# First stage of an encoder layer on one core: constant products ahead, squares behind the first parts, the norm's sums a block later

## The chip, the core and the metric

The kernel runs on one core of a Trainium2 chip. Its engines run at the same time and wait for each other through semaphores: TensorE (PE in the views, with its weight loads as PEld), VectorE (DVE), ScalarE (ACT), GpSimd (POOL) and SyncE (SP), which issues nearly all transfers. The metric is the time of one execution on the device in microseconds (us); lower is better.

## What is computed

One layer of a hybrid encoder on x of 1024 frames by 1024 features, in float32. The start of it is all that this study needs:

```python
h = rmsnorm(x, norm_mix_g[li])          # x * rsqrt(mean(x*x) + EPS) * gain
z = h @ w_in[li]
qa, fa, ia, ga, qb, kb, vb, gate_a, gate_b = jnp.split(z, split_at, axis=-1)
oa = hgrn2_mixer(qa, fa, ia, ga, lower_bounds[li], hgrn_onorm_g[li])
ob = band_attention(qb, kb, vb, ...)
```

Behind it follow the two branches' projections, a SwiGLU block and a gated embedding, which the change leaves as they are.

## The kernel before

x lies with its features on the 128 partitions: eight chunks of 128 features by 1024 frames. Every float32 factor of a large product is cut in two parts, a first part `hi` (rounded, from ACT) and a rest `lo` (the value minus its first part, from DVE for x, from POOL for weights), and a product is made of three: hi x hi, lo x hi and hi x lo. A weight tile of 128 x 1024 passes through `unit` and `unit_piece`: load into a raw buffer (two of them), cast on ACT (`wh`), subtraction on POOL (`wl`); four pairs of `wh` and `wl` go round, and a new tile must wait until TensorE has left the oldest.

`first_norm` is the first stage. It loads the eight chunks and two weight tiles (of q and f of the first head), the tiles in two pieces of 256 and 768 columns. For each chunk ACT makes the first part scaled by the norm's gain (`self.A.activation`), DVE the rest (`split`, L194; for the first chunk in two halves, L281). The norm's own factor, one number per frame, is not needed yet: it is put on the results afterwards. For it ACT squares each chunk in place (`norm_feed`) and DVE adds the squares up in `self.acc` (L204). TensorE makes 8 chunks x 4 results x 3 = 96 products of 512 columns, chunk by chunk, into four banks of PSUM (`outs`), whose pool has eight.

`hgrn_in(0, outs)` follows. Its eight token blocks of 24 products each (256 columns, PE tiles `pm<-wh,s` and `pm<-wl,s`) take two further weight tiles (`in_tm`). `norm_sums` sums `acc` over the partitions with 8 products against a column of ones, DVE scales, and POOL takes the power -1/2 (L215), which gives `self.r`, one factor per frame. Each block's result is then scaled by `r` (L338 and L340 on DVE, L339 on ACT), which frees its bank. `norm_rows` spreads `r` over the partitions with 8 products against the unit matrix, ACT copies them to `rb`, and `rows_out` scales the four waiting results. `near` then makes products of q and f which the mixer needs behind the next head's first products.

The order on each engine is the order in which the code issues, arranged by a scheduler for DVE, POOL and ACT where the code doesn't pin it (`Pinned`, `order`): TensorE, SP and the instructions sent through `self.A`, `self.V` and `self.G` are pinned. Helpers record one line for all that they issue: L81 is every product of `mul`, L76 every load, L52 every pinned instruction, L121 and L124 the cast and the subtraction of `unit_piece`.

Of the kernel before, what the change touches and what calls it, by code (L numbers as in the profile page):

```python
# [13 lines left out]
AF = mybir.ActivationFunctionType  # L14
ALU = mybir.AluOpType
AX = mybir.AxisListType

P = 128
# [8 lines left out]

SLOTS = 32
LATE = 8
FIRST = 4  # L30
RING = 4
RAW = 2
# [7 lines left out]
def f32(ap):  # L40
    return ap.bitcast(F32)
# [13 lines left out]
class Trunk:  # L55
# [205 lines left out]
    def first_norm(self):  # L261

        nc = self.nc
        self.u = []
        outs = [self.mm() for _ in range(4)]
        start = [self.unit() for _ in range(2)]
        ws = [(hi, lo) for hi, lo, _, _ in start]
        for k in range(KC):
            x = self.slot()
            sc = self.cols[:, C_MIX + k:C_MIX + k + 1]  # L270
            if k == 0:

                hi, lo = self.slot(F32R), self.slot(F32R)
                h0, h1 = slice(0, HALF), slice(HALF, T)
                self.load(x[:, h0], self.d["x"][k][:, h0])
                for unit in start:
                    self.unit_piece(unit, 0, 2 * P)
                self.load(x[:, h1], self.d["x"][k][:, h1])
                for h in (h0, h1):
                    self.A.activation(hi[:, h], x[:, h], AF.Copy, scale=sc)  # L280
                    nc.vector.scalar_tensor_tensor(lo[:, h], x[:, h], sc, f32(hi[:, h]), ALU.mult, ALU.subtract)  # L281
                self.u.append((hi, lo))
            else:
                self.load(x, self.d["x"][k])
                self.u.append(self.split(x, sc, self.A))
            if k == 1:
                for unit in start:
                    self.unit_piece(unit, 2 * P, D)
            if k == 3:
                self.load(self.eye, self.d["eye"])  # L290
                self.load(self.masks, self.d["masks"])
            if k:
                self.norm_feed(prev, k == 1, prev, act=self.A)
            prev = x
        self.norm_feed(prev, False, prev, act=self.A)
        self.lower_bound()
        pairs = [self.feature_pairs(ws[i // 2], self.u, i % 2) for i in range(4)]
        for k in range(KC):
            for i in (0, 2, 1, 3):
                ah, al, bh, bl = pairs[i][k]  # L300
                self.mul(outs[i], ah, bh, start=k == 0, stop=False)
                self.mul(outs[i], ah, bl, start=False, stop=False)
                self.mul(outs[i], al, bh, start=False, stop=k == KC - 1)
        return outs


    def hgrn_in(self, h, outs=None):

        nc = self.nc
        q, f, v, g = self.hg[h] = [self.slot() for _ in range(4)]  # L310

        def rows_out(j, half, ps):
            hs = slice(half * HALF, half * HALF + HALF)
            if j == 0:
                nc.vector.scalar_tensor_tensor(q[:, hs], ps, 128.0 ** -0.5, self.rb[:, hs], ALU.mult, ALU.mult)
            else:
                nc.vector.tensor_tensor(f[:, hs], ps, self.rb[:, hs], ALU.mult)
                nc.scalar.activation(f[:, hs], f[:, hs], AF.Sigmoid)
                nc.vector.tensor_scalar(f[:, hs], f[:, hs], self.lb1[:, h:h + 1], self.lb[:, h:h + 1], ALU.mult, ALU.add)

        if outs is None:
            for j in range(2):
                (w,) = self.weights()
                for half in range(2):
                    ps = yield from self.feature(w, self.u, half, piece=3)
                    rows_out(j, half, ps)
                    yield 1296
            near = self.near(h)
        else:
            near = iter(())  # L330
        ws = self.weights(2)
        for b in range(8):
            ps = yield from self.token(ws, b, 256, piece=4)
            if outs is not None and b == 0:
                self.norm_sums()
            bs = slice(b * P, b * P + P)
            r = self.r[:, b:b + 1]
            nc.vector.tensor_scalar(v[:, bs], ps[:, :P], r, None, ALU.mult)  # L338
            nc.scalar.activation(g[:, bs], ps[:, P:256], AF.Sigmoid, scale=r)  # L339
            nc.vector.scalar_tensor_tensor(g[:, bs], ps[:, P:256], r, g[:, bs], ALU.mult, ALU.mult)  # L340
            if outs is not None and b == 1:
                self.norm_rows()
                for i in range(4):
                    rows_out(i // 2, i % 2, outs[i])
                near = self.near(h)
            next(near, None)
            yield 1296

    def near(self, h):

        nc = self.nc
        q, f = self.hg[h][:2]
        kt = self.slot()
        self.V.tensor_scalar(kt, f, -1.0, 1.0, ALU.mult, ALU.add)
        parts = []

        def product(a, b, tag):
            hi, lo = [self.small(HALF, F32R, tag=tag, shape=(P, HALF if tag == "qk" else 640)) for _ in range(2)]
            raw = self.small(640, tag="s")
            self.V.tensor_tensor(raw[:, :HALF], a, b, ALU.mult)  # L360
            parts.append((hi[:, :HALF], lo[:, :HALF], raw[:, :HALF]))

        def part(hi, lo, raw):
            nc.scalar.copy(hi, raw)
            nc.gpsimd.tensor_tensor(lo, raw, f32(hi), ALU.subtract)

        for i in range(2):
            hs = slice(i * HALF, i * HALF + HALF)
            product(kt[:, hs], q[:, hs], "qk")
        yield  # L370
        for i in range(2):
            part(*parts[i])
        yield
        self.V.tensor_tensor(q, q, f, ALU.mult)
        yield
        qv, kv = (t[:, :].rearrange("p (j two) -> p j two", two=2) for t in (q, kt))
        product(kv[:, :, 0], qv[:, :, 1], "bias")
        yield
        yield
        part(*parts[2])  # L380
        self.hg[h] += [kt, parts]
# [248 lines left out]
    def attention(self):  # L630
# [32 lines left out]

        for i in range(FIRST, 8):
            next(feed, None)
            if i == FIRST:
                self.hgrn_gate()
# [809 lines left out]
    def run(self):  # L1477
# [16 lines left out]
        with ExitStack() as es:  # L1494
# [13 lines left out]
            with ExitStack() as mixer:  # L1508
# [5 lines left out]
                self.feed = self.attn_in()  # L1514
                weave(chain(self.attn_v(), islice(self.feed, FIRST)), self.hgrn_mix(3), 41500 + 1300 * FIRST, 17000)
                self.attn_setup()
# [11 lines left out]
            with ExitStack() as xs:  # L1528
                self.late = xs.enter_context(tc.tile_pool(name="late", bufs=LATE, reuse_waits="tile"))
                self.sq = Small(tc, xs, {"square": 1}, "out_", reuse_waits="tile")  # L1530
# [29 lines left out]
def drain(stream):  # L1560
    while True:
        try:
            next(stream)
        except StopIteration as e:
            return e.value


def weave(main, side, main_ns, side_ns):

    done = {id(main): 0, id(side): 0}  # L1570
    live = {id(main): (main, main_ns), id(side): (side, side_ns)}
    while live:
        i = min(live, key=lambda i: done[i])
        stream, whole = live[i]
        got = next(stream, None)
        if got is None:
            del live[i]
        else:
            done[i] += max(got, 50) / whole
# [94 lines left out]
```

## Time and profile before

| what | value |
|---|---|
| three runs | 1618.75 us median, 1617.07 to 1619.6 |
| the profiled execution | 1616.41 us, its span 1614.6 us |
| TensorE busy | 1592.5 us, 99% of the span |
| DVE, ACT, POOL busy | 1095.5, 589.6, 677.2 us |
| mean granted TensorE clock | 0.998 |

The span runs from the first to the last instruction of the profiled execution; the time beside it holds 1.8 us more, for what lies around the program. The profiled execution is 2.3 us below the median of the three runs, so a sum made from its trace gives a difference, which is then taken from the median. Matmuls are pipelined: the time from start to start tells their pace, their own length is longer.

### The profile page before, as it was taken

Reading aid. Unit: us, or ns where it says so; the run is one execution under the profiler, and the core shown is the slowest. Engines: PE = TensorE matmul, PEld = TensorE weight load, DVE = VectorE, ACT = ScalarE, POOL = GpSimd, SP = SyncE. Lnnn points to the kernel's source line nnn. Section 1 sums busy time; section 2 is a strip of 40 time slices with the busy share of each in tenths; the row PEclk is TensorE's granted clock in tenths of the full one; section 3 lists DMA queues with packets and bytes.
Section 4 is the critical chain, followed back from the end, with each engine's and each line's share of the span. In section 5 each row is a group of like instructions: output and inputs, shape, how many; then the busy total and the mean of one; then the engine's idle time right before and its main releaser. Section 6 shows DMA issues by size and latency. Waiting matters only on the chain.

```text
span 1614.6 us, 21560 instructions
## 1 busy us (share of the span) xinstructions
PE 1592.5 (99%) x8356; PEld 1333.0 (83%) x8356; DVE 1095.5 (68%) x1706; ACT 589.6 (37%) x999; POOL 677.2 (42%) x362
## 2 busy tenths in 40 slices
PE   8999999999999999999999999999999999999998
PEld 6998998878888888888887788888888888888887
DVE  5656655389897443334988888888888856437653
ACT  5221121277776311121466423222222235336321
POOL 3422221313122122125322777777777765546320
PEclk9999999999999999999999999999999999999999
DMA  5101000200103475733343432232333277655511
GB/s 188 53 27 53 27 27 27 85 1 27 60 14 107 152 235 185 257 133 131 105 143 145 147 114 98 98 98 98 107 103 113 82 271 281 211 195 176 196 72 53
DMA packets 64471, 189.62 MB, mean 117 GB/s; under 512 B 7280, under 2 KB 8048, under 8 KB 62448
## 3 DMA queue, kind: packets, MB, share of 16 engines
q1 hardware_dynamic: 64224, 188.22, 33.9%
q8 instruction: 66, 1.08, 0.3%
q14 instruction: 37, 0.30, 0.1%
q10 hardware_dynamic: 144, 0.02, 0.0%
HBM read 139.71 MB, written 48.50 MB: 117 GB/s over the span
## 4 chain that ended last, share of the span: by engine, by line
PE 83%; DVE 8%; ACT 2%; DMA 1%; issue 1%; POOL 1%; SPq 0%; DVEq 0%; ACTq 0%; POOLq 0%
PE pm L81 80%; DVE s L52 5%; PE pm L84 3%; DVE m L52 2%; ACT s L52 1%; POOL wl L124 1%; DMA wr<-in_sg 0%; DMA wr<-d 0%; ACT wh L121 0%; DVE q L52 0%; DMA wr<-in_su 0%; DVE wl L124 0%; ACT m L52 0%; DMA wr<-in_qk 0%; POOL m L547 0%
## 5 line engine op out<-in xcount | busy, mean ns | idle before, releaser
L81 PE MATMUL pm<-s,wh 128*128 128x512 f32 (+1 forms) x2136 | 659.8, 390 | 6.2 <-ACT wh L121 5.1
L124 POOL TENSOR_TENSOR wl<-wr,wh 128x1024 fp32r<-128x1024 f32 (+2 forms) x114 | 285.0, 2504 | 533.7 <-ACT wh L121 526.1
L81 PEld LDWEIGHTS pm<-s,wh 128*128 128x128 f32 x2136 | 398.2, 188 | 89.0 <-ACT wh L121 5.1
L81 PE MATMUL pm<-s,wl 128*128 128x512 f32 (+1 forms) x1068 | 415.0, 389 | 0.5 <-POOL wl L124 0.5
L81 PE MATMUL pm<-s,whi 128*128 128x512 f32 x1232 | 386.0, 394 | 5.1 <-ACT whi L52 2.1
L81 PEld LDWEIGHTS pm<-s,whi 128*128 128x128 f32 x1232 | 233.0, 189 | 58.6 <-ACT whi L52 2.6
L52 DVE TENSOR_TENSOR s<-s,s 128x512 f32<-128x512 f32 (+3 forms) x172 | 208.4, 1238 | 76.8 <-ACT s L52 42.1
L121 ACT CAST wh<-wr 128x1024 fp32r<-128x1024 f32 (+2 forms) x120 | 121.3, 1011 | 377.4 <-PE pm L81 188.3
L81 PE MATMUL pm<-s,wlo 128*128 128x512 f32 x616 | 243.3, 395 | 0.3 <-DVE wlo L52 0.3
L81 PE MATMUL pm<-wh,s 128*128 128x256 f32 (+1 forms) x896 | 238.2, 340 | 0.0
L81 PEld LDWEIGHTS pm<-s,wl 128*128 128x128 f32 x1068 | 200.7, 188 | 42.7 <-POOL wl L124 1.4
L81 PEld LDWEIGHTS pm<-wh,s 128*128 128x128 f32 x896 | 154.5, 190 | 13.9 <-DVE s L340 0.2
L81 PE MATMUL pm<-wl,s 128*128 128x256 f32 (+1 forms) x448 | 147.5, 329 | 0.8 <-POOL wl L124 0.8
L81 PEld LDWEIGHTS pm<-s,wlo 128*128 128x128 f32 x616 | 116.6, 189 | 27.2 <-DVE wlo L52 0.7
L52 DVE TENSOR_TENSOR s<-pm,s 128x512 f32<-128x512 f32 x101 | 65.7, 686 | 81.0 <-PE pm L81 81.0
L52 POOL TENSOR_TENSOR s<-s,t 128x512 f32<-128x512 f32 x44 | 75.5, 1716 | 89.8 <-ACT t L52 89.8
L52 DVE TENSOR_TENSOR t<-pm,t 128x512 f32<-128x512 f32 x106 | 72.8, 687 | 53.1 <-PE pm L81 50.0
L52 ACT CAST whi<-q 128x512 fp32r<-128x512 f32 (+1 forms) x63 | 47.8, 759 | 155.3 <-DVE q L52 133.2
L52 POOL TENSOR_TENSOR wlo<-wr,whi 128x512 fp32r<-128x512 f32 (+1 forms) x46 | 93.2, 2033 | 25.8 <-ACT whi L52 25.1
L81 PEld LDWEIGHTS pm<-wl,s 128*128 128x128 f32 x448 | 85.3, 191 | 6.3 <-POOL wl L124 1.0
L52 ACT CAST s<-s 128x1024 fp32r<-128x1024 f32 x70 | 69.1, 1004 | 57.6 <-DMA s<-d 23.2
L547 POOL TENSOR_TENSOR m<-m,mhalf 128x8 f32<-128x8 f32 x16 | 26.6, 1664 | 122.8 <-DVE m L52 122.7
(136 smaller groups left out, 1881.2 us busy)
## 6 DMA issues: line engine op xcount, KB each, us to landing
s<-d SPq DMA_DIRECT2D x51, 512.0 KB, 5.0
d<-s SPq DMA_DIRECT2D x87, 256.0 KB, 2.5
d<-dq SPq DMA_DIRECT2D x60, 256.0 KB, 4.6
wr<-d SPq DMA_DIRECT2D x28, 512.0 KB, 3.6
wr<-in_fm SPq DMA_DIRECT2D x22, 512.0 KB, 3.5
dq<-in_wq SPq DMA_DIRECT2D x11, 1024.0 KB, 7.1
wr<-in_sg SPq DMA_DIRECT2D x22, 512.0 KB, 3.9
wr<-in_su SPq DMA_DIRECT2D x22, 512.0 KB, 4.3
```

Source lines behind the costliest of these rows:

```text
L52: return lambda *a, **k: self.trunk.order(op(*a, **k), self.key)
L81: return self.order(self.nc.tensor.matmul(*a, **k))
L84: return self.order(self.nc.tensor.transpose(*a, **k))
L121: self.nc.scalar.copy(hi[:, c], raw[:, c])
L124: rest.tensor_tensor(lo[:, c], raw[:, c], f32(hi[:, c]), ALU.subtract)
L547: nc.gpsimd.tensor_tensor(ss, ss, self.mhalf[:, 0:8], ALU.pow)
```

## The change

Three things change, all in the first 60 us. Ahead of everything TensorE issues 18 products of a constant tile of ones (128 columns each) into a bank of their own. The squares and their adds are issued behind all eight first parts and rests, and the load, cast and subtraction of the next two weight tiles (`weights(0, ahead=2)`) ahead of them. In `hgrn_in(0, outs)` the sums of the norm are issued behind token block 1 in place of block 0, the scaling of blocks 0 and 1 behind that, and the norm's rows behind block 3 in place of block 1; the steps of `near`, one for each block from there, are emptied at the end.

```diff
+IDLE = 18
@@ first_norm
-        self.u = []
+        self.u, xs = [], []
+        idle = self.mm()
+        for _ in range(IDLE):
+            self.mul(idle[:, :P], self.onesr, self.onesr, start=True, stop=True)
         outs = [self.mm() for _ in range(4)]
...
-            if k:
-                self.norm_feed(prev, k == 1, prev, act=self.A)
-            prev = x
-        self.norm_feed(prev, False, prev, act=self.A)
+            xs.append(x)
+        self.weights(0, ahead=2)
+        for k, x in enumerate(xs):
+            self.norm_feed(x, k == 0, x, act=self.A)
         self.lower_bound()
@@ hgrn_in
         ws = self.weights(2)
+        made = []
         for b in range(8):
             ps = yield from self.token(ws, b, 256, piece=4)
-            if outs is not None and b == 0:
+            if outs is not None and b == 1:
                 self.norm_sums()
-            bs = slice(b * P, b * P + P)
-            r = self.r[:, b:b + 1]
-            nc.vector.tensor_scalar(v[:, bs], ps[:, :P], r, None, ALU.mult)
-            nc.scalar.activation(g[:, bs], ps[:, P:256], AF.Sigmoid, scale=r)
-            nc.vector.scalar_tensor_tensor(g[:, bs], ps[:, P:256], r, g[:, bs], ALU.mult, ALU.mult)
-            if outs is not None and b == 1:
+            made.append((b, ps))
+            while made and (outs is None or b > 0):
+                n, ps = made.pop(0)
+                bs = slice(n * P, n * P + P)
+                r = self.r[:, n:n + 1]
+                nc.vector.tensor_scalar(v[:, bs], ps[:, :P], r, None, ALU.mult)
+                nc.scalar.activation(g[:, bs], ps[:, P:256], AF.Sigmoid, scale=r)
+                nc.vector.scalar_tensor_tensor(g[:, bs], ps[:, P:256], r, g[:, bs], ALU.mult, ALU.mult)
+            if outs is not None and b == 3:
                 self.norm_rows()
                 for i in range(4):
                     rows_out(i // 2, i % 2, outs[i])
                 near = self.near(h)
             next(near, None)
             yield 1296
+        drain(near)
```

Nine lines came in ahead, so a line number of the kernel before is up to nine higher in the changed one (L81 is L82, L124 is L125).

On ACT, from the second chunk's first part on, the kernel before has this order (an ACTIVATE with `cols` is a first part, one with the same tile on both sides a square, a CAST that of a weight):

```order
L52 ACTIVATE s_140<-s_138,cols 128x1024
L52 ACTIVATE s_123<-s_123 128x1024
L121 CAST wh_118<-wr_119 128x768
L121 CAST wh_121<-wr_122 128x768
L52 ACTIVATE s_153<-s_151,cols 128x1024
L52 ACTIVATE s_138<-s_138 128x1024
L52 ACTIVATE s_161<-s_159,cols 128x1024
```

The changed kernel has there:

```order
L53 ACTIVATE s_159<-s_157,cols 128x1024
L122 CAST wh_137<-wr_138 128x768
L122 CAST wh_140<-wr_141 128x768
L53 ACTIVATE s_171<-s_169,cols 128x1024
L53 ACTIVATE s_177<-s_175,cols 128x1024
```

The squares left these places; they stand behind the last first part, the two full-width casts among them:

```order
L53 ACTIVATE s_203<-s_201,cols 128x1024
L53 ACTIVATE s_142<-s_142 128x1024
L122 CAST wh_208<-wr_209 128x1024
L53 ACTIVATE s_157<-s_157 128x1024
L122 CAST wh_214<-wr_215 128x1024
L53 ACTIVATE s_169<-s_169 128x1024
```

On DVE the rests (SCALAR_TENSOR_TENSOR) and the adds (TENSOR_TENSOR into the first chunk's tile) of the first stage take turns in the kernel before:

```order
L194 SCALAR_TENSOR_TENSOR s_141<-s_138,cols,s_140 128x1024
L194 SCALAR_TENSOR_TENSOR s_154<-s_151,cols,s_153 128x1024
L204 TENSOR_TENSOR s_123<-s_123,s_138 128x1024
L194 SCALAR_TENSOR_TENSOR s_162<-s_159,cols,s_161 128x1024
L204 TENSOR_TENSOR s_123<-s_123,s_151 128x1024
L194 SCALAR_TENSOR_TENSOR s_172<-s_169,cols,s_171 128x1024
```

In the changed kernel the last two rests, the seven adds' first and last, and what follows stand like this:

```order
L195 SCALAR_TENSOR_TENSOR s_198<-s_195,cols,s_197 128x1024
L195 SCALAR_TENSOR_TENSOR s_204<-s_201,cols,s_203 128x1024
L205 TENSOR_TENSOR s_142<-s_142,s_157 128x1024
L205 TENSOR_TENSOR s_142<-s_142,s_169 128x1024
...
L205 TENSOR_TENSOR s_142<-s_142,s_201 128x1024
L214 TENSOR_SCALAR m_442<-pm_433 128x8
L346 TENSOR_SCALAR s_363<-pm_383,m_444 128x128
L346 TENSOR_SCALAR s_363<-pm_408,m_444 128x128
```

All adds come behind all rests now, and the scaling of two blocks behind the sums. On POOL the power of the norm (the row with `mhalf`) stands in the kernel before between the token blocks' weights and the next head's:

```order
L124 TENSOR_TENSOR wl_334<-wr_336,wh_335 128x1024
L124 TENSOR_TENSOR wl_340<-wr_342,wh_341 128x1024
L215 TENSOR_TENSOR m_400<-m_398,mhalf 128x8
L124 TENSOR_TENSOR wl_346<-wr_348,wh_347 128x1024
L124 TENSOR_TENSOR wl_352<-wr_354,wh_353 128x1024
```

and in the changed one behind both of the next head's subtractions:

```order
L125 TENSOR_TENSOR wl_207<-wr_209,wh_208 128x1024
L125 TENSOR_TENSOR wl_213<-wr_215,wh_214 128x1024
L125 TENSOR_TENSOR wl_365<-wr_367,wh_366 128x1024
L125 TENSOR_TENSOR wl_371<-wr_373,wh_372 128x1024
L216 TENSOR_TENSOR m_444<-m_442,mhalf 128x8
```

TensorE's order moves only as the diff says, and SP's loads keep theirs.

## Rows read from the trace of the kernel before

**Rows 1.** Waits of TensorE, 0 to 61 us: us in total, times, longest.

```profile
PE pm L81 <- ACT wh L121: 5.1, 1, 5.1
...
PE pm L81 <- DVE s L194: 1.1, 3, 0.5
```

**Rows 2.** Timeline of TensorE, 5 to 20 us: start, us, instruction, [idle before, releaser].

```profile
11.24 0.50 PE L81 MATMUL pm<-s,wh 128*128 128x512 f32 x1 [0.49 <-DVE s L194]
...
14.70 0.50 PE L81 MATMUL pm<-s,wh 128*128 128x512 f32 x1 [0.45 <-DVE s L194]
...
16.40 0.50 PE L81 MATMUL pm<-s,wl 128*128 128x512 f32 x1 [0.49 <-POOL wl L124]
...
18.68 0.50 PE L81 MATMUL pm<-s,wh 128*128 128x512 f32 x1 [0.17 <-DVE s L194]
```

**Rows 3.** Timeline of TensorE, 31.5 to 63 us, the token blocks and what follows.

```profile
32.19 0.28 PE L81 MATMUL pm<-wh,s 128*128 128x256 f32 x1
...
34.73 0.39 PE L81 MATMUL pm<-wl,s 128*128 128x256 f32 x1 [0.83 <-POOL wl L124]
...
36.16 1.84 PE L81 MATMUL pm<-ones,s 128*128 128x1 f32 x16
37.86 0.36 PE L81 MATMUL pm<-wh,s 128*128 128x256 f32 x1
...
40.81 1.95 PE L81 MATMUL pm<-eye,m 128*128 128x128 f32 x16
...
62.23 1.10 PE L81 MATMUL pm<-m,onesr 128*128 128x512 f32 x4
```

**Rows 4.** Timeline of ACT, first parts (with cols), a square, casts.

```profile
8.71 1.15 ACT L52 ACTIVATE s<-s,cols 128x1024 fp32r<-128x1024 f32 x1 [0.52 <-DMA s<-in_x]
9.77 1.04 ACT L52 ACTIVATE s<-s 128x1024 f32<-128x1024 f32 x1
10.72 1.55 ACT L121 CAST wh<-wr 128x768 fp32r<-128x768 f32 x2
12.18 1.15 ACT L52 ACTIVATE s<-s,cols 128x1024 fp32r<-128x1024 f32 x1
```

**Rows 5.** Timeline of DVE: a rest (L194), two adds (L204), a block's last scaling (L340).

```profile
13.36 1.29 DVE L194 SCALAR_TENSOR_TENSOR s<-s,cols,s 128x1024 fp32r<-128x1024 f32 x1 [2.17 <-ACT s L52]
14.56 2.87 DVE L204 TENSOR_TENSOR s<-s,s 128x1024 f32<-128x1024 f32 x1
...
20.88 1.21 DVE L204 TENSOR_TENSOR s<-s,s 128x1024 f32<-128x1024 f32 x1
...
42.39 0.34 DVE L340 SCALAR_TENSOR_TENSOR s<-pm,m,s 128x128 f32<-128x128 f32 x1
```

**Rows 6.** Timeline of POOL, pieces of it: subtractions, the power, parts for the mixer.

```profile
13.41 2.94 POOL L124 TENSOR_TENSOR wl<-wr,wh 128x768 fp32r<-128x768 f32 x1
...
27.74 3.62 POOL L124 TENSOR_TENSOR wl<-wr,wh 128x1024 fp32r<-128x1024 f32 x1 [11.39 <-ACT wh L121]
...
38.28 1.64 POOL L215 TENSOR_TENSOR m<-m,mhalf 128x8 f32<-128x8 f32 x1 [3.60 <-DVE m L213]
39.88 2.37 POOL L124 TENSOR_TENSOR wl<-wr,wh 128x1024 fp32r<-128x1024 f32 x1
...
49.96 3.53 POOL L365 TENSOR_TENSOR m<-m,m 128x512 fp32r<-128x512 f32 x2 [4.44 <-ACT m L364]
```

**Rows 7.** Transfers issued at 4.00 and at 16.38: KB, us to landing.

```profile
s<-in_x SPq DMA_DIRECT2D x1, 512.0 KB, 7.8
...
wr<-in_tm SPq DMA_DIRECT2D x1, 512.0 KB, 4.8
```

**Rows 8.** Busy us (instructions) by engine, granted clock, DMA; and TensorE's timeline there.

```profile
5.77:9.18 3.41, 3.41 (x8) 1.80 (x7) 0.75 (x1) 1.59 (x3) 1.15 (x2) 1.00 0.98 389
...
862.50:865.90 3.40, 3.35 (x8) 2.67 (x9) 2.08 (x3) 3.40 (x6) 0.00 (x0) 0.50 0.80 317
...
861.52 0.74 PE L81 MATMUL pm<-s,whi 128*128 128x512 f32 x2 [2.11 <-ACT whi L52]
```

## The prediction

> **What bounds the kernel now.** I read the view of waits first, for TensorE alone and the first 61 us: it stands still for others in three lines of that view, 5.1 us before its first product and 2.4 behind it (the first and the last of the three: [rows 1]), and the whole program has little more to give, since TensorE is busy 99% of the span. The change touches nothing behind the eighth token block, so its worth is decided by what TensorE waits for until about 60 us. Its timeline tells which instruction is late [rows 2, 3]. Behind the first product come four places: at 11.24 the rest (low part) of the second x chunk, at 14.70 that of the third, at 16.40 the rest of a weight tile from POOL, at 18.68 the rest of the fourth chunk. From 18.68 to the first token product at 32.19 there are 11 + 48 = 59 products in 13.51 us, 0.229 each, with no wait. The fifth place is 34.73, a weight rest again. Token block 0 therefore takes 36.16 - 32.19 = 3.97 us, but block 1 takes 40.81 - 37.86 = 2.95: that wait costs 1.02.
>
> Then I asked why those parts are late. ACT alternates first parts and squares, with the casts of weights between them [rows 4]. DVE alternates rests and adds [rows 5]. Both are paced by more than arrival: the third chunk was issued at 4.00 and landed 7.8 us later, at 11.8 [rows 7], but its first part began at 12.18. The last thing to see is that DVE and POOL stop each other. A free add takes 1.21; the add at 14.56 took 2.87 and ended at 17.43, 1.08 after POOL's subtraction of 13.41 (2.94 long) ended; that subtraction itself began under DVE's rest of 13.36 and ended 1.70 behind that rest's end at 14.65. In the same way the full-width subtraction at 27.74 took 3.62 beside adds, where a free one takes 2.37 [rows 5, 6]. So of a DVE instruction with two SBUF inputs and a POOL subtraction one stands still until the other ends, and where both have work they take turns.
>
> **The change, part by part.**
>
> *The 18 constant products.* They need only the constant tile, and the trace has them start at about 1.1 us at the earliest. Their price: 128 columns are a quarter of a 512-column product, which goes every 0.43 us at the low clock (8 in 3.40 us where the granted clock was 0.50, [rows 8]; the first stage has 8 in 3.41 too until 9.2, though its column says 1.00), so 0.11 each and 1.9 us together; the dearer bound is the fp32 rows product, 16 passes of 128x128 in 1.95 us [rows 3], 0.12 each, doubled for the clock: 4.4 us, ended at 5.5. I take the lower half, ended before the first product at 5.1. The later end delays the first product by 0.4, and the wait at 11.24 hides that. [...] But the second product of chunk two waits for DVE until 11.24 whatever ran before, and that rest hangs on the landing of x (ACT's first part starts at 8.71 with a wait for the DMA [rows 4]). [...]
>
> [...]
>
> *Squares behind all first parts.* Without the square at 9.77, ACT's two 768-wide casts start 0.95 earlier (9.77 for 10.72). The third chunk's first part then starts with its landing, 11.87 for 12.18, and DVE's rest could start at 13.05 for 13.36. But POOL moves as well. Its first 768-wide subtraction is asked for at 10.66, finds DVE in the second chunk's rest until 11.18, and ends about 1.70 later (16.35 - 14.65, the same operation once released, [rows 5, 6]), at 12.9. Its second one follows at once, about 0.1 ahead of DVE's 13.05. Taking turns as above, POOL then holds until 14.7 and the rest of chunk three ends about 15.85 (1.29 less the 0.13 by which a released add is shorter). TensorE's second product of the chunk goes at 15.90, not 14.70. From there 11 + 60 = 71 products of 0.229 run without a wait, since the later rests are early now: 16.26, and the token blocks start at 32.16 for 32.19. The stall at 16.40 and 18.68 has become one at 15.90. Gain 0.03.
>
> *weights(0, ahead=2) ahead of the squares.* The full-width weights (loads issued at the same places; the later landed 4.8 us after 16.38, at 21.2 [rows 7]) are cast on ACT among the first squares, at about 20.8 and 22.6. POOL's subtractions run about 22.0 to 24.3 and 25.4 to 27.6, not from 27.74 on, so the wait at 34.73 goes: 1.02.
>
> *The adds.* All seven now run behind the rests, from 22.8 on, each waiting for the one before it and sharing with POOL: the first ends 25.4, the second 28.7, then four at 1.3 until 33.95. POOL's next weight waits for TensorE to leave its buffer (about 0.9 before the token start, so 31.7), is cast by ACT in about 1.05 and asks at 33.0. It gets in behind the sixth add, 33.95 to 36.2, and the last add ends 37.3. The norm's sums come behind two token blocks now, at 32.16 + 2 x 2.95 = 38.06: not held. The order of add six (asks 32.8) and that subtraction is close; this is the fragile step.
>
> *Sums and rows later.* POOL's power, now queued behind that weight's and the next one's subtraction (37.3 to 39.55), is asked for at about 40: 1.64 later, 41.7, as in [rows 5, 6]. Block 0's bank was free 2.8 behind the power's end (42.39 + 0.34 against 38.28 + 1.64), with block 1's two evictions some 0.7 behind: 44.5 and 45.2 now. The rows want the banks, one after the other, from 38.06 + 1.70 + 2 x 2.95 = 45.7 on and have them. The products of near() are wanted 13.5 us behind the rows (62.23 against 40.81 + 1.95 = 42.76 is 19.5 with two more blocks between, 5.9); before, POOL's second part was done 10.7 behind the rows, at 53.49 [rows 6]. Hidden, with 2.8 to spare.
>
> **Sum.** 0.03 + 1.02 = 1.05 us. The profiled execution took 1616.41 (span 1614.6), 2.34 under the median of 1618.75; against its own time the changed kernel comes out at 1615.4, against the median at **1617.7**. A difference under 0.2% (3.2 us) cannot be told from none here.
>
> **Rivals.**
> - *DVE goes first in chunk three* (its rest at 13.05 to 14.33, POOL 14.33 to 16.04). The sixth product then waits to 16.09, 67 more take 15.34, and the token blocks start 31.4. TensorE's buffer is free sooner, POOL's weight asks at 32.25, before add six, and both full subtractions get between the adds: the last ends 39.3. The sums are wanted at 37.3 and wait 2.0. Before, sums behind two blocks would have stood at 36.16 + 2.95 = 39.11, so this loses 0.2: 1618.95. For it: the two requests lie within 0.1 us.
> - *No turn-taking worth naming:* chunk three's rest at 14.33, product at 14.38, 71 x 0.229 later the tokens at 30.64, both waits gone: gain 1.55 + 1.02 = 2.6, 1616.2. Against it: every overlap of the two in [rows 5, 6].
> - *Slower: the sums' wait and the clock.* Place: the sums behind block 1. Where TensorE stood 2.11 us at 861.52, the granted clock was 0.50 next and 8 products took 3.40 instead of 1.8 [rows 8], 1.6 lost. After a wait of 2 for the adds that makes 0.2 + 1.6, 1620.6. It is a loss once the last add ends after 39.11 and shows as slower after 42.35, or 40.7 with the clock.
> [...]
>
> [...]
>
> **How the numbers follow.** Forecast 0.42, first rival 0.26, no turns 0.14, slower 0.10, constant products 0.08. Four of five lie within 2.6 below and 1.9 above the median; executions of this kernel alone spread from 1617.07 to 1619.6, which widens both ends by about 1: 1614.8 to 1620.6. Faster by over 0.2% needs "no turns" or paying products with luck in the spread: 0.12. Slower needs the clock to fall and the adds to end later still: 0.07. Within: 0.81.
>
> **What would show it.** Right: a wait of about 1.8 in the third chunk near 15.9 for DVE, none at 16.40, 18.68 and 34.73; POOL's second 768-wide subtraction uninterrupted; token blocks from 32.2; sums at 38.1 without a wait; the block behind the rows 1 us earlier than its old place. Wrong: the rest of chunk three ending at 14.4; a wait in front of the sums; a granted clock of 0.50 in the first 50 us; first products at 0.23 with the 11.24 wait gone.

## The result, and the profile after

The changed kernel takes **1621.0 us** (median of 15 runs, 1619.37 to 1623.92) where the kernel before takes 1618.05 in the same session: a ratio of 1.0018, with a 95% interval of 1.0011 to 1.0025. It is about 2.9 us slower. The forecast was 1617.7 in a range up to 1620.6, so it had the wrong sign and the range missed the time by 0.4 us. Three executions on record ran far longer than the others of their kernels (1753.74 us of the changed kernel, 2259.35 of the kernel before, 3215.17 of the squares alone); medians and ratios here leave them out.

TensorE's timeline of the changed kernel, at the places of [rows 1 to 3] (start, us, instruction, idle before it and releaser):

```profile
1.17 4.10 PE L82 MATMUL pm<-onesr 128*128 128x128 f32 x18 [1.17 <-DVE onesr L239]
5.19 1.38 PE L82 MATMUL pm<-s,wh 128*128 128x512 f32 x2
...
15.47 0.50 PE L82 MATMUL pm<-s,wh 128*128 128x512 f32 x1 [1.58 <-DVE s L195]
...
31.73 0.28 PE L82 MATMUL pm<-wh,s 128*128 128x256 f32 x1
...
39.09 1.95 PE L82 MATMUL pm<-ones,s 128*128 128x1 f32 x16 [1.44 <-DVE s L205]
...
49.93 0.36 PE L82 MATMUL pm<-wh,s 128*128 128x256 f32 x1
...
68.44 0.74 PE L82 MATMUL pm<-s,s 128*128 128x64 f32 x5 [1.21 <-DVE s L53]
```

The first half is as forecast: one wait in the third chunk, none at the old places of 16.40, 18.68 and 34.73 [rows 2, 3], token blocks from 31.73. Then the norm's sums wait 1.44 us, and at 68.44 the mixer's products wait 1.21. What the sums wait for is seen on DVE and POOL. DVE's timeline (the first add, the sixth, the sixth and seventh together, and the first of VectorE's two products at the mixer):

```profile
22.43 2.59 DVE L205 TENSOR_TENSOR s<-s,s 128x1024 f32<-128x1024 f32 x1 [1.03 <-ACT s L53]
...
32.46 3.25 DVE L205 TENSOR_TENSOR s<-s,s 128x1024 f32<-128x1024 f32 x1
...
32.46 6.58 DVE L205 TENSOR_TENSOR s<-s,s 128x1024 f32<-128x1024 f32 x2
...
65.48 2.21 DVE L53 TENSOR_TENSOR s<-s,s 128x512 f32<-128x512 f32 x1
```

POOL's timeline (the first of the two subtractions that stand between the adds, both together, the power, the two subtractions at the mixer), and ACT's cast for the first one:

```profile
32.20 2.42 POOL L125 TENSOR_TENSOR wl<-wr,wh 128x1024 fp32r<-128x1024 f32 x1 [4.92 <-ACT wh L122]
32.20 5.75 POOL L125 TENSOR_TENSOR wl<-wr,wh 128x1024 fp32r<-128x1024 f32 x2 [4.92 <-ACT wh L122]
41.32 1.64 POOL L216 TENSOR_TENSOR m<-m,mhalf 128x8 f32<-128x8 f32 x1 [3.37 <-DVE m L214]
62.37 4.77 POOL L125 TENSOR_TENSOR wl<-wr,wh 128x1024 fp32r<-128x1024 f32 x2
...
31.07 1.06 ACT L122 CAST wh<-wr 128x1024 fp32r<-128x1024 f32 x1 [2.04 <-issue]
```

POOL asked at 32.20, 0.26 ahead of add six, and add six stood until the subtraction ended at 34.62; POOL's second one stood until add six ended, and add seven until that ended. The last two adds took 6.58 us instead of 2.5, and the last ended at 39.04. Behind the sums, which had waited, TensorE's clock fell. By windows of the span (busy us and instructions of PE, PEld, DVE, ACT, POOL; granted clock; DMA):

```profile
31.80:39.10 7.30, 5.86 (x50) 5.65 (x48) 7.03 (x3) 1.28 (x2) 5.75 (x2) 1.00 0.20 73
40.98:44.40 3.42, 3.42 (x18) 3.42 (x18) 1.02 (x5) 0.98 (x1) 1.64 (x1) 0.50 0.00 0
44.40:50.00 5.60, 5.60 (x50) 5.60 (x49) 1.98 (x7) 2.25 (x6) 0.00 (x0) 1.00 0.01 4
```

At 0.50 token products stand 0.213 us apart instead of 0.120: 16 steps in 3.42 us (the row also counts those that reach in at its ends), each 0.093 dearer, lose 1.5 us.

### The profile page after: what moved, and what is told of

It is laid out like the page before. It is cut to its first block, busy times and chain, and to the rows that moved or that the text cites. A ratio compares the mean times of both kernels' runs of the same rounds, so it can differ in the third digit from the quotient of the medians.

```text
span 1619.8 us, 21598 instructions
## 1 busy us (share of the span) xinstructions
PE 1596.0 (99%) x8374; PEld 1337.9 (83%) x8374; DVE 1101.8 (68%) x1706; ACT 589.5 (36%) x999; POOL 676.3 (42%) x362
## 4 chain that ended last, share of the span: by engine, by line
PE 80%; DVE 8%; DMA 3%; POOL 2%; ACT 2%; issue 1%; SPq 0%; DVEq 0%; ACTq 0%; POOLq 0%
PE pm L82 77%; DVE s L53 5%; PE pm L85 3%; DVE m L53 1%; DMA wr<-d 1%; DMA s<-d 1%; POOL wl L125 1%; ACT s L53 1%; POOL s L53 0%; DMA wr<-in_sg 0%; ACT wh L122 0%; DMA wr<-in_su 0%; DVE q L53 0%; DVE wl L125 0%; SPq L77 0%
## 5 line engine op out<-in xcount | busy, mean ns | idle before, releaser
L82 PE MATMUL pm<-s,wh 128*128 128x512 f32 (+1 forms) x2136 | 659.3, 390 | 1.6 <-DVE s L195 1.6
L125 POOL TENSOR_TENSOR wl<-wr,wh 128x1024 fp32r<-128x1024 f32 (+2 forms) x114 | 284.2, 2497 | 529.7 <-ACT wh L122 511.9
L82 PEld LDWEIGHTS pm<-s,wh 128*128 128x128 f32 x2136 | 398.7, 188 | 83.8 <-DVE s L195 2.3
L82 PE MATMUL pm<-s,wl 128*128 128x512 f32 (+1 forms) x1068 | 415.2, 389 | 0.6 <-POOL wl L125 0.6
L82 PE MATMUL pm<-s,whi 128*128 128x512 f32 x1232 | 385.1, 394 | 8.1 <-DVE s L53 3.7
L82 PEld LDWEIGHTS pm<-s,whi 128*128 128x128 f32 x1232 | 232.2, 189 | 61.4 <-issue 3.1
L82 PE MATMUL pm<-s,wlo 128*128 128x512 f32 x616 | 242.5, 394 | 0.3 <-DVE wlo L53 0.3
L82 PE MATMUL pm<-wh,s 128*128 128x256 f32 (+1 forms) x896 | 239.6, 342 | 0.0
L82 PEld LDWEIGHTS pm<-s,wl 128*128 128x128 f32 x1068 | 201.0, 188 | 42.6 <-POOL wl L125 1.4
L82 PEld LDWEIGHTS pm<-wh,s 128*128 128x128 f32 x896 | 155.8, 192 | 13.6
L82 PE MATMUL pm<-wl,s 128*128 128x256 f32 (+1 forms) x448 | 148.1, 331 | 0.0
L82 PEld LDWEIGHTS pm<-s,wlo 128*128 128x128 f32 x616 | 116.2, 189 | 27.1 <-DVE wlo L53 0.7
L82 PEld LDWEIGHTS pm<-wl,s 128*128 128x128 f32 x448 | 86.2, 192 | 5.3
```

Source lines behind the costliest of these rows:

```text
L82: return self.order(self.nc.tensor.matmul(*a, **k))
L125: rest.tensor_tensor(lo[:, c], raw[:, c], f32(hi[:, c]), ALU.subtract)
```

## The experiments

Each run has 11 timings unless said otherwise; ratios are against the kernel before on the same chip, with their 95% interval. "Pinned" means that an instruction is issued through an object that keeps the order of the code on its engine.

**The constant products left out** of the changed kernel:

```diff
-        idle = self.mm()
-        for _ in range(IDLE):
-            self.mul(idle[:, :P], self.onesr, self.onesr, start=True, stop=True)
```

> The changed kernel without the 18 constant products. Theory A (the last add of x's squares ends late, the norm's sums wait 1.4 us for it, and TensorE's granted clock falls behind that wait): nothing changes, the first product of x keeps its place, the sums still wait about 1.4 us, the clock still shows 0.50 near 41 to 44 us, and the time is the changed kernel's, about 2.9 us over the kernel before. Theory B (the constant products, by what they do to the clock, are what the loss hangs on): no 0.50 near 41 us, and the time is back within 0.5 us of the kernel before.

1621.35 us, 1.0018 (1.0009 to 1.0027): the same as with them, with the wait of the sums (1.5 us) and a clock of 0.50 from 43.0 to 46.4:

```profile
43.01:46.42 3.41, 3.41 (x18) 3.41 (x18) 1.02 (x5) 1.85 (x3) 1.08 (x1) 0.50 0.01 2
```

Theory B is out.

**The constant products alone**, added to the kernel before (the same lines with +):

> The kernel before with the 18 constant products ahead and nothing else. Theory A (they bring nothing and cost nothing): the same within 0.5 us, the first product of x at 5.1 to 5.2. Rival (the clock rises earlier with them on the mean over executions): 0.5 to 1 us faster.

1618.74 us, 0.9997 (0.9988 to 1.0006): nothing gained, nothing lost.

**The squares, adds and weights alone**, sums and rows at their old place:

```diff
+            xs.append(x)
+        self.weights(0, ahead=2)
+        for k, x in enumerate(xs):
+            self.norm_feed(x, k == 0, x, act=self.A)
```

> The kernel before with the squares and adds of x behind all its first parts and the next weights asked for ahead of them, but no constant products, and the sums behind block 0, the rows behind block 1, as before. Theory A: the wait at 34.73 goes; the adds end at 35 (if the sums' block comes ahead of POOL's next subtractions) to 39 us, the sums are wanted near 35 and wait 1 to 4 us, the granted clock falls to 0.50 behind them: 2 to 4 us slower than the kernel before. Rival (the loss of the changed kernel belongs to its later sums and rows): no more than 1 us slower.

1625.82 us (5 timings), 1.0043 (1.0030 to 1.0056), which is 7.0 us. Theory A in direction; the size is above its range of 2 to 4, for the sums wait 4.27 us and the clock stays low twice as long, from 39.71, still in that wait, to 46.54. TensorE's timeline, and the window:

```profile
39.99 0.80 PE L81 MATMUL pm<-ones,s 128*128 128x1 f32 x3 [4.27 <-DVE s L204]
...
39.71:46.54 6.83, 6.55 (x30) 6.55 (x31) 0.99 (x5) 0.60 (x1) 1.64 (x1) 0.50 0.23 77
```

So the squares' new place by itself costs more than the whole change, and the later sums win part of it back.

**The sums and rows later, alone** (behind blocks 1 and 3, in the kernel before):

```diff
-            if outs is not None and b == 0:
-                self.norm_sums()
...
+            if outs is not None and b == 1:
+                self.norm_sums()
...
+            if outs is not None and b == 3:
```

> The kernel before with the norm's sums moved behind block 1 and the rows behind block 3, nothing else. Theory A: the adds are all done by 32.4 us as before, so the sums (wanted near 39) wait for nothing and the clock does not fall there; the block behind the rows stands within 0.2 us of the kernel before. The later rows push the chain of the mixer on VectorE by two blocks, so that the wait near 67 to 68 us grows from 0.34 us to about 1.2: about 0.9 us slower in all. Rival (the later sums and rows by themselves cost the whole loss): 2 us or more slower.

1618.49 us, 1.0005 (0.9996 to 1.0014): not to be told from none, but the trace has the place. The sums wait for nothing. At the mixer VectorE's two products on 128x512 take 2.79 us where they took 1.94 in the kernel before, because POOL's third part ends at 61.2 and its two subtractions stand over 1.6 us of them (64.26 to 65.89), in the kernel before over 0.8 (64.11 to 64.90). TensorE's waits to 75 us, DVE's and POOL's timeline, and a window behind; then the same places in the kernel before (DVE, POOL, TensorE):

```profile
PE pm L81 <- DVE s L52: 1.2, 1, 1.2
...
64.26 2.79 DVE L52 TENSOR_TENSOR s<-s,s 128x512 f32<-128x512 f32 x2
...
61.13 4.76 POOL L124 TENSOR_TENSOR wl<-wr,wh 128x1024 fp32r<-128x1024 f32 x2
...
69.29:72.70 3.41, 3.41 (x10) 2.64 (x9) 3.27 (x5) 0.00 (x0) 0.00 (x0) 0.50 0.00 0
...
64.11 1.94 DVE L52 TENSOR_TENSOR s<-s,s 128x512 f32<-128x512 f32 x2
...
60.14 4.76 POOL L124 TENSOR_TENSOR wl<-wr,wh 128x1024 fp32r<-128x1024 f32 x2 [4.07 <-ACT wh L121]
...
66.19 0.30 PE L81 MATMUL pm<-s,s 128*128 128x64 f32 x1 [0.34 <-DVE s L52]
```

**Only the weights earlier**, in the kernel before:

```diff
+            if k == 6:
+                self.weights(0, ahead=2)
```

> The kernel before with one call added: the next two weight tiles are asked for while the seventh chunk of x is taken in, so that only the wait of TensorE at 34.73 us should go. Squares, adds, sums and rows stay where they were. Theory A: that wait (1.02 us) goes, its cast and subtractions run between the last chunks' parts, and the time is 0.5 to 1.0 us under the kernel before. Rival (the subtraction, now between the adds, holds those up as in the changed kernel, and the sums behind block 0 wait instead): a wait at the sums near 36 us and no gain, or a loss of 1 us and a fall of the clock.

1620.58 us, 1.0012 (1.0003 to 1.0021): the rival. The wait for the weight's rest goes, but POOL's two subtractions (6.96 us from 26.07) now run among the last rest and the last adds, the last two adds take 6.84 us from 30.70, and the sums behind block 0 wait for those. TensorE's timeline and the window behind it:

```profile
37.59 0.61 PE L81 MATMUL pm<-ones,s 128*128 128x1 f32 x4 [1.10 <-DVE s L204]
...
38.43:45.25 6.82, 6.82 (x33) 6.82 (x34) 1.11 (x5) 1.65 (x2) 3.08 (x2) 0.50 0.28 103
```

So from this place in the code the 1.02 us of [rows 3] cannot be had: moving POOL's work moves the stall into the adds. No other place was tried.

**POOL's late subtractions behind the sums.** A first try only moved the call in the code:

```diff
-        ws = self.weights(2)
+        ws = self.weights(2, ahead=AHEAD if outs is None else 0)
...
                 self.norm_sums()
+                self.weights(0, ahead=AHEAD)
```

> The changed kernel, with POOL's next full-width weight subtractions (those that ran at 32.2 and 34.6 us between the adds) asked for behind the norm's sums. Theory A: the last add ends near 35 instead of 39.0, the sums at about 37.6 do not wait, no granted clock of 0.50 follows, and the block behind the rows stands about 1.4 us earlier than in the kernel before instead of 1.3 later; with 0.9 us given back at the mixer's wait near 68 us the time is about 0.5 us under the kernel before, some 3 under the changed kernel. Rival (the clock falls at that place whatever the sums wait for, or the loss comes later): the 0.50 stays and the time is the changed kernel's within 1 us.

1620.43 us, 1.0021 (1.0012 to 1.0030), with the same wait of 1.4 us: the scheduler put the subtractions ahead of the power all the same (POOL's two run from 33.17 to 38.92 in this trace), so the run says nothing on the theory. Pinned, the order holds:

```diff
-        rest = ... else self.nc.gpsimd
+        rest = ... else self.G if self.pin else self.nc.gpsimd
...
+                self.pin = True
                 self.norm_sums()
+                self.weights(0, ahead=AHEAD)
+                self.pin = False
```

> The changed kernel, with POOL's queue now written out at this place: the power of the norm, then the two full-width subtractions that ran at 32.2 and 34.6 us between the last adds. Theory A (the loss is the wait of the sums, 1.4 us, for adds that POOL's subtractions hold up, and the fall of TensorE's clock behind that wait): the last two adds take 1.2 us each, the last ends near 35, the sums (wanted near 37.7) wait for nothing, no granted clock of 0.50 shows between 38 and 47 us, and the time is 2.5 to 3 us under the changed kernel, 1618 to 1618.5, with the wait of about 1.2 us at the mixer near 68 us still there. Rival (the clock falls behind the 16 small passes of the sums whatever stands before them): the wait goes but the 0.50 stays, 1619.5 or so.

1619.92 us, 1.0010 (1.0001 to 1.0019). The mechanism is as theory A has it: the adds take 1.23 each, the sums wait for nothing, and the clock stays. Less came of it than expected (1618 to 1618.5), and this time alone is not to be told from the changed kernel's, whose interval overlaps. The trace is of one of the two fastest executions (1617.86), so what the others lose beside is not seen; what it does show is a new wait in front of the rows. DVE's, POOL's and TensorE's timeline, and a window:

```profile
31.91 3.89 DVE L205 TENSOR_TENSOR s<-s,s 128x1024 f32<-128x1024 f32 x3
...
42.55 1.83 DVE L529 TENSOR_TENSOR m<-m 128x8 f32<-128x8 f32 x1
44.41 2.31 DVE L530 TENSOR_SCALAR m<-m 128x8 f32<-128x8 f32 x1
46.64 0.59 DVE L351 SCALAR_TENSOR_TENSOR s<-pm,m,s 128x128 f32<-128x128 f32 x2
...
41.95 4.74 POOL L53 TENSOR_TENSOR wl<-wr,wh 128x1024 fp32r<-128x1024 f32 x2
...
47.08 1.13 PE L82 MATMUL pm<-eye,m 128*128 128x128 f32 x8 [1.16 <-POOL wl L53]
...
38.00:50.00 12.00, 10.85 (x93) 10.67 (x92) 7.11 (x12) 3.61 (x7) 6.34 (x3) 1.00 0.26 89
```

The same two operations in the changed kernel:

```profile
43.52 0.16 DVE L526 TENSOR_TENSOR m<-m 128x8 f32<-128x8 f32 x1
43.71 0.17 DVE L527 TENSOR_SCALAR m<-m 128x8 f32<-128x8 f32 x1
```

The two 128x8 operations square the norm for the attention, which comes later. Beside POOL they take 1.83 and 2.31 us, where the changed kernel has them without POOL at 0.16 and 0.17, and the evictions that free the rows' banks stand behind them. (The profile names POOL for the wait: its subtractions end at 46.69, VectorE's second operation at 46.72.)

**Those two operations moved** (`self.V` keeps the code's order on VectorE, and there they stand with the attention):

```diff
-        nc.vector.tensor_tensor(self.r64, self.r, self.r, ALU.mult)
-        nc.vector.tensor_scalar(self.r64,
+        self.V.tensor_tensor(self.r64, self.r, self.r, ALU.mult)
+        self.V.tensor_scalar(self.r64,
```

> The kernel with POOL's queue written out, and with the two operations on 128x8 that square the norm for the attention (they ran at 42.5 and 44.4 us, 1.83 and 2.31 us long beside POOL's subtractions, ahead of the evictions) moved to where the attention is built. Theory A (those two, held by POOL, hold VectorE's evictions of the token blocks, and so the banks that the rows want): the wait of 1.16 us in front of the rows goes, and the time is about 1.1 us under the kernel with only POOL's queue written out; the wait of about 1.5 at the mixer near 67 us stays or grows. Rival (the evictions are late for the norm's power anyway): the wait stays within 0.3 us.

1618.07 us, 0.9996 (0.9987 to 1.0005) where the run without has 1.0010: the wait in front of the rows is gone, that at the mixer stays. This interval lies wholly under the changed kernel's (1.0011 to 1.0025): with POOL's order pinned and these two moved, the loss is gone. The waits to 75 us:

```profile
PE pm L82 <- DVE s L53: 1.2, 1, 1.2
PE pm L82 <- DVE onesr L239: 1.2, 1, 1.2
PE pm L82 <- DVE s L195: 0.5, 1, 0.5
```

**The rows behind block 2** instead of 3 (`b == 3` to `b == 2`), first with the two operations in place, then with them moved:

> The kernel with POOL's queue written out, and the rows behind block 2 instead of block 3. Theory A (the rows two blocks later push VectorE's chain of the mixer, which costs 0.9 us at the wait near 68 us): the rows come 2.95 us earlier, the power of the norm is done in time, the wait near 68 us goes back from 1.2 us to about 0.3, and the time is about 0.9 us under the kernel with the rows behind block 3, so 1617.2 to 1617.6, at or a little under the kernel before. Rival (that wait comes from something else, such as POOL's subtractions standing beside the mixer's products): it stays at 1.2, and nothing is gained.

1621.59 us, 1.0019 (1.0010 to 1.0028). The mixer's wait fell to 0.3 as theory A has it, but the same two operations now hold the rows 3.0 us, and the clock fell behind that (48.2 to 51.6): what was won at one place was lost at another.

```profile
46.97 0.60 PE L82 MATMUL pm<-eye,m 128*128 128x128 f32 x3 [3.01 <-DVE s L351]
```

> The same with the rows behind block 2. Theory A: the wait of 3.01 us in front of the rows, seen with the rows there and the 128x8 operations in place, goes to under 0.4; no granted clock of 0.50 between 38 and 55 us; the wait at the mixer near 67 us is about 0.3 as in the kernel before; TensorE stands about 2 us earlier at 70 us than in the second profile of the kernel before, and the time is 1.5 to 2.2 us under the kernel before, a ratio of 0.9986 to 0.999. Rival (the mixer's wait comes back, since its operands follow POOL's next subtractions): 0.9 us of it is lost.

1617.53 us, 0.9996 (0.9987 to 1.0004). The waits are as expected but for 0.6 us at the rows, and yet the ratio misses the 0.9986 to 0.999 that was expected: at the mixer TensorE stands 0.33 us earlier than in the second profile of the kernel before (66.48 for 66.81), not about 2. The time is 0.5 us under the kernel with the rows behind block 3, a difference that the intervals do not show.

**One rest of the first weights on VectorE**, again in both states:

```diff
-                for unit in start:
-                    self.unit_piece(unit, 2 * P, D)
+                self.unit_piece(start[0], 2 * P, D)
+                self.by_turns, self.turn = True, 0
+                self.unit_piece(start[1], 2 * P, D)
+                self.by_turns = False
```

> The last kernel, with the 768-wide rest of the second first-stage weight on VectorE instead of POOL. Theory A (VectorE's rest of the third chunk takes 2.69 us instead of 1.29 because POOL's second 768-wide subtraction runs first): TensorE's wait of 1.58 us in the third chunk shrinks to about 0.9, since VectorE does that rest itself (about 0.9 us) before its chunk; everything behind stands 0.7 us earlier, 1616.5 to 1617. Rival (the third chunk is then held by VectorE's extra work as long as it was by POOL): no difference.

1620.10 us, 1.0008 (0.9999 to 1.0017), 1.5 under the kernel without it, and not the 1616.5 to 1617 expected: the third chunk has no wait now, but the kernel without the edit had only 0.25 there in its trace, and the 3.0 us at the rows stay.

The edit does more than its name says. It sets the counter `self.turn` to 0, and the output projection (`out_proj`), which gives its weights' rests to the two engines in turn by that counter, now starts with the other one: between 700 and 900 us seven full-width rests run on VectorE, six in the other kernels. All fourteen traces without the edit at a full granted clock have a wait of TensorE for ACT between 861 and 871 us, of 1.9 to 3.5 us; the three with it have none there. The first line is of the next kernel's trace below, the second and third are of the trace without the edit (rows behind block 2, operations moved):

```profile
L125 DVE TENSOR_TENSOR wl<-wr,wh 128x1024 fp32r<-128x1024 f32 x7 | 8.5, 1217 | 0.0
...
L125 DVE TENSOR_TENSOR wl<-wr,wh 128x1024 fp32r<-128x1024 f32 x6 | 11.1, 1850 | 2.0 <-ACT wh L122 2.0
...
862.97 0.73 PE L82 MATMUL pm<-s,whi 128*128 128x512 f32 x2 [2.39 <-ACT whi L53]
```

> The same with the 768-wide rest of the second first-stage weight on VectorE. Theory A: TensorE has no wait in the third chunk (as seen once: no wait there over 0.2 us, 0.5 us gained), so about 0.5 us under the kernel without it: 2.0 to 2.7 us under the kernel before, a ratio of 0.9983 to 0.9988. Rival: the token blocks start earlier, ask for the sums earlier, and wait for the adds, which end at 35.8; no gain.

**1615.93 us, 0.9979 (0.9970 to 0.9988)**: faster than both kernels, with no wait over 0.62 us between the first product of x and 75 us and no fall of the clock there. It is 1.6 us under the kernel without the edit where 0.5 was expected; in the two traces the same products stand 0.8 us earlier by 206 us and 2.3 earlier by 935 us, so the larger part arises where the side effect lies, and no run has the third chunk's part alone. Its waits to 75 us, DVE's timeline in the third chunk, and the window that held the loss:

```profile
PE pm L82 <- DVE onesr L239: 1.2, 1, 1.2
PE pm L82 <- DVE s L353: 0.6, 1, 0.6
PE pm L82 <- ACT s L53: 0.3, 1, 0.3
PE pm L82 <- DVE s L53: 0.3, 1, 0.3
...
12.02 2.18 DVE L125 TENSOR_TENSOR wl<-wr,wh 128x768 fp32r<-128x768 f32 x1 [0.33 <-ACT wh L122]
14.12 1.27 DVE L195 SCALAR_TENSOR_TENSOR s<-s,cols,s 128x1024 fp32r<-128x1024 f32 x1
...
31.00:70.00 39.00, 38.05 (x282) 35.86 (x281) 25.82 (x42) 11.98 (x20) 15.88 (x8) 1.00 0.16 55
```

> The same without the 18 constant products. Theory A (they bring nothing, because TensorE's clock rises between 8.7 and 14.2 us with them, between 8.9 and 14.7 without): the same time within 0.5 us. Rival (the clock rises earlier with them, on the mean over runs): 0.5 to 1 us slower than with them.

1616.46 us, 0.9984 (0.9975 to 0.9992): inside the other's interval. The constant products can stay or go.

**Both kernels again**, unchanged, for a second profile:

> The kernel before, unchanged, for a second profile beside the one of the rows. Its time is that of the kernel before within 0.5 us. What it tells: which of the differences seen so far lie between two executions of one kernel. Theory A expects no granted clock of 0.50 between 30 and 70 us and waits of 0.8 at the weight's rest near 35 and 0.3 near 66 us again; the stretches of 0.50 near 860 to 910 us, and the time at which the clock first rises (9.2 us in the first profile, 14.5 to 14.7 in two kernels that only reorder later work), may stand elsewhere.

1617.54 us, 0.9996 (0.9987 to 1.0004). Its profile took 1618.2 us where the first took 1616.41, with the same code. From 9.5 to 13.4 us the first execution (first line) ran 15 of TensorE's products, the second 10:

```profile
9.50:13.40 3.90, 3.41 (x15) 2.49 (x14) 1.32 (x2) 3.90 (x6) 1.79 (x1) 1.00 1.04 415
...
9.50:13.40 3.90, 3.90 (x10) 3.04 (x10) 1.32 (x2) 3.90 (x5) 1.22 (x1) 1.00 1.04 415
```

The clock's record begins at 9.18 us in the first and at 13.43 in the second, and up to there products of 512 columns stand 0.43 apart. The sum's basis was an execution in which the clock rose early. By the norm's sums the second stands 0.62 us behind (36.78 for 36.16), and the rest of the 1.8 comes later. In it the token weights are waited for 0.44 us at 35.36, not 0.83, so block 0 takes 3.57 us and the wait costs 0.62, not 1.02.

> The changed kernel, unchanged, for a second profile. In the first one 1.6 us of the loss against the second profile of the kernel before stood at 68 us, and 1.8 more came behind 860 us (waits near 872, 912 and 1350 us). Theory A (the change costs what stands at 68 us; the rest lies between executions): the sums wait 1.4 us again, the clock falls behind it again, TensorE stands 1.2 to 2.0 us later than in the second profile of the kernel before at 70 us (more where the clock first rises later), and the waits behind 860 us stand elsewhere or are gone. Rival (the later waits belong to the changed kernel): the same waits of 1.8 us near 912 and 0.65 near 1350 again.

1621.3 us (10 timings), 1.0015 (1.0006 to 1.0024): the changed kernel's time holds. Its trace has a granted clock of 0.85 where the others have 1.00, so its times are not set beside theirs. One thing in it bears on the argument: the sums, wanted later, waited for nothing, and the clock fell behind them all the same.

```profile
40.20 2.04 PE L82 MATMUL pm<-ones,s 128*128 128x1 f32 x16
...
43.32:46.74 3.42, 3.42 (x19) 3.42 (x18) 1.27 (x6) 1.91 (x3) 0.84 (x1) 0.50 0.03 7
```

> The changed kernel, unchanged, for a second undisturbed profile. Theory A: at 70 us TensorE stands 1.2 to 2.0 us later than in the second profile of the kernel before, and the waits of 1.8 us near 912 and of 0.65 us near 1350 stand elsewhere or are gone. Rival: the same two waits again.

One timing, 1619.47 us. The same products stand 1.43 us later than in the second profile of the kernel before behind the rows (50.69 for 49.26) and 2.36 later at the mixer (69.17 for 66.81; 1.2 to 2.0 was expected), with the sums' wait of 1.46 and a clock of 0.50 from 42.0 to 45.4. The wait near 912 us is 0.2 as in the kernel before and that near 1350 is gone. In the kernel with the constant products alone the one near 912 stands again, at 1.8 us. So these two waits lie between executions, and what the traces show of the change's cost is made before 70 us, as theory A has it. (Over the whole span these two traces end 1.3 us apart, since stretches of low clock behind 860 us fall differently too.)

## Why the prediction was wrong

**Right in effect, wrong in price: the constant products.** Forecast 1.9 to 4.4 us, taken the lower; measured 4.10, 18 products 0.213 apart, twice the quarter of a 512-column product that the sum went by. It cost nothing all the same: the first product of x came at 5.19. By the time of the run with these products alone, 0.9997, they gave nothing. The chance of 0.08 that they pay was the author's estimate of what an earlier rise of the clock would bring, and no run shows that they bring one: the first rise stood at 9.18 and 13.43 in the kernel before, at 10.26 and 14.70 in the changed one.

**Right: the third chunk and the token weights.** POOL went first, DVE's rest took 2.69 us and TensorE waited until 15.47 (forecast 15.90); the token blocks began at 31.73 (32.16) without the wait of 34.73. Part of that is the execution: in the last profile of the changed kernel, where the clock rose at 14.70 and not at 10.26, the third chunk has no wait and the token blocks begin at 32.47.

**Wrong: the adds.** The step that failed is "the order of add six (asks 32.8) and that subtraction is close; this is the fragile step", with POOL asking at 33.0. It asked at 32.20, and add six at 32.46. Most of the 0.8 us is a slip: 0.9 ahead of 32.16 is 31.3, not 31.7, and with a cast of 1.05 the sum itself gives 32.3, ahead of add six (even 31.7 and 1.05 make 32.75, not 33.0); the tokens' earlier start and the measured lead of the cast (31.07 against 31.73) make up the last 0.1. With POOL first, both subtractions stand between the last adds, the last ends at 39.04 instead of 37.3, and the sums, wanted at 37.65, wait 1.44. The consequence, adds ending at 39.3, stood in the first rival; the whole course, a wait of the sums and a fall of the clock that ends at 1620.6, was the slower rival, at a chance of 0.10. Pinning POOL's order shows the cause: with the adds free both wait and fall are gone, and with the 128x8 operations moved as well the loss is gone from the time (0.9996). POOL asked at 32.20, VectorE at 32.46, and POOL's subtraction ran at once (2.42 us) while the add took 3.25: a sum that hangs on 0.3 us hung here on who asked first.

**Wrong: "Hidden, with 2.8 to spare."** The products of 62.23 [rows 3] were indeed not late. The ones behind them were: POOL's parts for the mixer push its next subtractions to 62.37 from 60.14, while TensorE is only 1.4 us behind there (63.60 for 62.23), so they stand on VectorE's work for the mixer, and TensorE waits 1.21 instead of 0.34. I had checked the first product that needs the rows and stopped there. Moving sums and rows alone shows the same wait.

**The sum, mended** with what the first pair of traces shows: the sums are wanted at 37.65, 1.46 ahead of the 39.11 of the kernel before (the forecast had 1.05), so -1.46 + 1.44 (sums) + 1.5 (clock) + 0.87 (mixer) = +2.35 us. The first product of the mixer stands 2.25 later (68.44 for 66.19), and 2.36 in the second pair (the second profile of the kernel before, the last of the changed one). The times differ by 2.9, with 1.8 to 4.0 in the interval; where the remaining half of a us lies is not shown.

**The range.** Its text widens both ends by about 1, but 1620.6 is the slower rival's own time, not widened. With the 1 us the range would have held the result, by width and not by mechanism.

**Not settled:** what decides whether the clock falls behind a wait of about 1.2 us. At the mixer it fell in two kernels (the sums and rows alone, at 69.29; the 128x8 operations moved, at 67.9), not in the changed kernel, and not behind 1.49 us there with only POOL's order pinned. At the sums it fell in all six traces at a granted clock of 1.00 that show a wait there (1.10 to 4.27 us), and in none of that clock without one; but in the trace at 0.85 it fell there without a wait. So the wait goes with the fall and goes away with it, and what else can bring a fall stays open.

## What to carry to other kernels

Where instructions of two engines hold each other up, as POOL's subtractions and VectorE's adds did here (two adds in 6.58 us instead of 2.5), work out who asks first at every meeting, with the sum's own times; where the two lie within a few tenths of a us, price both orders and pin the cheaper one rather than forecast it. A helper engine's work that was moved out of one stall landed in another queue here (POOL's, out of the wait of 0.83 at 34.73 and into waits of 1.44 at the sums and 1.21 at the mixer): follow it to the next two consumers, not one. Take two profiles of the kernel before: two executions of the same code stood 0.6 us apart by the sums and 1.8 at the end, more than the forecast gain. And see what else an edit changes: a counter that two stages share moved work nearly 800 us later.

## What the hardware showed unexpectedly

- Beside POOL's subtractions VectorE's small operations stood still too: with POOL's order pinned, 128x8 with two SBUF inputs took 1.83 us (0.16 in the changed kernel, where POOL is idle), 128x8 with one SBUF input and an immediate 2.31 us (0.17 there). An eviction that reads PSUM ran in 0.35 beside one (43.43 in the kernel before, POOL's subtraction from 43.11 to 45.52).
- The constant products of 128 columns stood 0.213 us apart ahead of the clock's first rise, half of the 0.43 of the 512-column products there and not a quarter: as much as a token product of 256 columns at a granted clock of 0.50.
- The first rise of TensorE's clock moved between 8.7 and 14.7 us over the traces, with the constant products and without, and for one kernel between executions: 9.18 and 13.43 for the kernel before, 10.26 and 14.70 for the changed one.
